# Moving the last flip of a projection next to another run of transposes, and putting the last rows' row sum on VectorE

## The chip, the cores and the metric

The kernel runs on one NeuronCore of a Trainium2 chip. The metric is the device time of one execution in microseconds, median over runs. Five engines work side by side, each through its own list of instructions in order: TensorE (PE, matmul), VectorE (DVE), ScalarE (ACT), GpSimd (POOL) and SyncE (SP, which issues most of the DMA transfers). They wait for one another by semaphores.

## The reference

A backbone of two layers over 512 tokens of width 1024, with 256 context tokens in front. Layer 0 mixes the tokens by bidirectional retention with 4 heads, layer 1 by a chunked gMLP; a final RMSNorm gives the output.

```
def rmsnorm(x, g):
    return x * rsqrt(mean(x * x, -1) + 1e-6) * g

for i in range(2):                       # 0: retention, 1: gMLP
    shift, scale, gate = split(silu(c) @ ada_w[i] + ada_b[i], 3)
    h = rmsnorm(x, norm_g[i]) * (1 + scale) + shift
    out = mixer_i(h, context)            # retention: (o_normed * silu(z)) @ w_out, o per head 512 wide
    x = x + gate * out
return rmsnorm(x, final_g)               # 512 x 1024
```

## The kernel before, in words

Every matrix product is done as three matmuls: each fp32 operand is split into a high and a low part, and `mm3` adds low x high, high x low and high x high in one PSUM tile. So there are 6820 matmul instructions.

Every engine operation goes through a recording class whose `call` stands in line 54, so nearly all rows of the profile bear the line L54; an operation is known by its engine and its tiles. The instructions stand on each engine in the order of the program text.

**PSUM.** `pt()` gives PSUM tiles (`pst`) from a set of six that are handed out in turn: the tile asked for now lies where the one asked for six calls earlier lay, and its first writer waits until the readers of that earlier one are done.

**The output projection of head 3** (`project_out`, called with `between=turned`, `prepare=prepare`, `then=half_sum`). The loop runs over two halves of the tokens (`hf`, 256 tokens each), four weight pieces (`c`) and two pieces of 128 output features each (`mi`; m = 2c + mi). Each m is one PSUM tile of 12 matmuls (`pst<-og,hl`), after which VectorE adds it, scaled by the gate, to the residual: `acc<-pst,gate,acc`. `og[hf]` is the head's gated output, transposed and split. For the first half it is ready when the loop begins; for the second half `flip()` makes it: 8 PE transposes of `gt` into two PSUM tiles, ScalarE's casts to the high part (`og<-pst`), and VectorE's two subtractions for the low part (`og<-pst,og`). In the kernel before, `flip()` stands ahead of c = 2 of the first half. `prepare()` stands right behind it in the text; it is elementwise work for layer 1's weights (`hl_e<-raw,hl_e` and `raw<-raw` on VectorE), with no matmul in it.

From c = 3 of the first half, `between(hf, c)` turns finished parts of the residual back to token rows: 8 PE transposes of `acc` into two PSUM tiles, whose squares ScalarE then sums (`junk<-pst`, `sums`) for layer 1's norm. These transposes need m = 0 to 3 of that half.

**The end.** The last matrix product is that of layer 1. Its last piece is row tile t = 3, columns 512 to 1023, and comes in two parts of 256 columns, c = 0 and 1. `last_part(t, c, pr)` adds each part to the residual, sums its squares for the RMSNorm, multiplies by the norm's weight (`fg`), and after c = 1 takes the root and the reciprocal, scales the tile's 1024 columns and stores them. `load` issues on SP's queue, `nc.scalar.dma_start` on ACT's.

Of the kernel before, what the change touches and what calls it, by code (L numbers as in the profile page):

```python
# [9 lines left out]
AF = mybir.ActivationFunctionType  # L10
ALU = mybir.AluOpType
# [15 lines left out]
HS = 256  # L27
# [40 lines left out]
def hybrid_kernel(ctx, tc, xT_d, cT_d, cv_d, sv_d, rows_d, ada0_d, adag_d, w_d, rope_d, dec_d, ws_d, id_d, out_d):  # L68
    nc = tc.nc
    pe, act, dve, sp = (Queue(tc, e) for e in (nc.tensor, nc.scalar, nc.vector, nc.sync))  # L70
# [11 lines left out]
    def st(shape, tag, dt=F32, bufs=1, name=None):  # L82
        return sb.tile(shape, dt, tag=tag, name=name or tag, bufs=bufs)
# [34 lines left out]
    def t2(name, shape=(P, 512), dt=F32):  # L118
        return st(list(shape), "t2", dt, bufs=T2, name=name)

    def pt(shape=(P, 512), tag="ps"):
        return ps.tile(list(shape), F32, tag=tag, name="pst", bufs=6 if tag == "ps" else 2)
# [3 lines left out]
    def mm3(out, l, r, first, last):  # L126
        (lh, ll), (rh, rl) = l, r
        mm(out, ll, rh, start=first, stop=False, skip_group_check=True)
        mm(out, lh, rl, start=False, stop=False, skip_group_check=True)
        mm(out, lh, rh, start=False, stop=last, skip_group_check=True)  # L130
# [13 lines left out]
    def load(dst, src):  # L144
        sp.dma_start(dst, src)
# [234 lines left out]
    def between_modes():  # L380

        pr = pt((P, P))
        mm(pr, ones, ones, start=True, stop=True)
# [678 lines left out]
    def aside(work):  # L1062
        return bound(lambda: next(work, None))

    def step():
        return aside(bg)
# [7 lines left out]
    def decay(h, tags=None):  # L1074

        if h == 1:
            xt, ct = st([P, XW], "s0", name="dt"), st([P, CW], "s2", name="dt")
        else:
            whole = st([P, TW], "dec", name="dt")
            xt, ct = whole[:, 0:XW], whole[:, XW:]  # L1080
        dts[h] = xt, ct
        if tags:
            tables[:] = [st([P, 768], tag, name="exps") for tag in tags]
            for t, parts in zip(tables, (((0, 384, 128), (2, 0, 384), (4, 256, 256)), ((2, 896, 128), (4, 512, 128), (0, 512, 512)))):
                o = 0
                for i, at, n in parts:
                    load(t[:, o:o + n], dec_d[i][:, at:at + n])
                    o += n
        yield
        up, down = tables  # L1090
        exp = lambda to, src, o: act.activation(to, src, AF.Exp, scale=lg[:, o + h:o + h + 1])
        free = lambda a, n: t2("de")[:, 0:n] if h == 2 else down[:, a:a + n]
        z = P * (NT - 1)
        exp(xt[:, z:z + P], up[:, 0:P], 0)
        m = free(z + 256, P)
        exp(m, down[:, z + 256:z + 256 + P], 4)
        dve.tensor_tensor(xt[:, z:z + P], xt[:, z:z + P], m, ALU.mult)
        dve.tensor_tensor(xt[:, z:z + P], xt[:, z:z + P], ident, ALU.add)
        exp(xt[:, 0:z], down[:, 256:256 + z], 4)
        exp(xt[:, z + P:], up[:, P:XW - z], 0)  # L1100
        yield
        exp(ct, up[:, P:], 0)
        for a, n in ((0, 512), (512, CW - 512)) if h == 2 else ((0, CW),):
            m = free(a, n)
            exp(m, down[:, a:a + n], 4)
            dve.tensor_tensor(ct[:, a:a + n], ct[:, a:a + n], m, ALU.add)
        act.activation(root, eps, AF.Sqrt)
        yield
# [10 lines left out]
    def load_qk(h):  # L1119
        tags = ODD if h in (1, 2) else EVEN  # L1120
        srcs = (k_d[h][0], q_d[h][0], k_d[h][1], kc_d[h], q_d[h][1])
        t = []
        for tag, src in zip(tags, srcs):
            t.append(st([P, 2, 2, HS], tag, F32R, name="qk"))
            load(f32(t[-1][:, 1]).rearrange("p a b -> p (a b)"), src)
            if len(t) % 2:
                yield
        qk[h] = (t[1], t[4]), (t[0], t[2]), t[3]
        for x in t:
            halves(x)  # L1130
            yield
# [28 lines left out]
    def load_v(h):  # L1160
        v = []
        for tag, src in zip(("oA11", "oS1", "oS2"), (*v_d[h], vc_d[h])):
            v.append(v_tile(h, tag))
            load(f32(v[-1][:, 1]), src)
            yield
        z = st([P, NT, 512], "oA22" if h == 1 else "oA12", name="z")
        for t in range(2):
            load(z[:, 2 * t:2 * t + 2, :], z_d[h][t])
        vv[h] = v, z
        yield  # L1170
        for x in v:
            halves(x)
            yield
# [283 lines left out]
    def project_out(ws, og, flip, parts, then=None, between=None, prepare=None):  # L1457
        for hf in range(2):
            sl = slice(hf * HS, hf * HS + HS)
            for c in range(4):  # L1460
                w = ws[c]
                if (hf, c) == (0, 2):
                    flip()
                    if prepare:
                        prepare()
                for work in parts:
                    aside(work)
                if then is None and (hf, c) in ((0, 3), (1, 0), (1, 2)):
                    step()
                for mi in range(2):  # L1470
                    m = 2 * c + mi
                    if between and mi == (hf == 1 and c < 2):
                        between(hf, c)
                    p = pt((P, HS))
                    for kk in range(4):
                        o = kk * 256 + mi * P
                        mm3(p, (w[:, 0, o:o + P], w[:, 1, o:o + P]), (og[hf][:, 0, kk, :], og[hf][:, 1, kk, :]), kk == 0, kk == 3)
                        if (hf, m, kk) == (0, 4, 1) and then is None:
                            between_modes()
                    dve.scalar_tensor_tensor(acc[:, m, sl], p, gate0[:, m:m + 1], acc[:, m, sl], ALU.mult, ALU.add)  # L1480
                    if then:
                        then(hf, m)
# [3 lines left out]
    flip, ss = attend_two(load_qk(1), load_v(1), decay(1, ("w3", "g1")), qs)  # L1486
# [9 lines left out]
    for work in own:  # L1496
        drained(work)
    project_out(wos.pop(2), og, flip, (decay(3), vs, qs))
    for c in range(4):
        nc.gpsimd.dma_start(acc[:, 2 * c:2 * c + 2, :], xT_d[:, 2 * c:2 * c + 2, :], accum_op=ALU.add)  # L1500
# [114 lines left out]
    def prepare():  # L1615
        Q.stage = 3
        Q.free += V1_SLOTS[len(W):] + [w for w in W if w not in Q.free]
        Q.pump()
        Q.upto(FIRST_V1 + 4)

    def turned(hf, c):
        first_half(hf, c)
        if hf == 1 and c >= 2:
            Q.upto(FIRST_V1 + 3 + c)

    project_out(wos.pop(HEADS - 1), og, flip, (), then=half_sum, between=turned, prepare=prepare)


# [45 lines left out]
    fg = st([P, D], "g0", name="fg")  # L1674
# [71 lines left out]
    def last_part(t, c, pr):  # L1746

        ss, o = ends[t]
        h = slice(512 + c * HS, 512 + c * HS + HS)
        s = o1[t][:, h]  # L1750
        dve.tensor_tensor(s, pr, s, ALU.add)
        act.activation(t2("junk1")[:, 0:HS], s, AF.Square, accum_out=ss[:, 1:2])
        if c == 0:
            dve.scalar_tensor_tensor(ss[:, 0:1], ss[:, 1:2], 1.0 / D, ss[:, 0:1], ALU.mult, ALU.add)
        dve.tensor_tensor(o[:, h], s, fg[:, h], ALU.mult)
        if c == 0:
            return
        rows = out_d[t * P:t * P + P, :]
        act.activation(ss[:, 1:2], ss[:, 1:2], AF.Sqrt, bias=ss[:, 0:1], scale=1.0 / D)
        dve.reciprocal(ss[:, 1:2], ss[:, 1:2])  # L1760
        act.activation(o[:, 768:], o[:, 768:], AF.Copy, scale=ss[:, 1:2])
        nc.scalar.dma_start(rows[:, 768:], o[:, 768:])
        for a in (slice(0, 384), slice(384, 768)):
            dve.tensor_scalar(o[:, a], o[:, a], ss[:, 1:2], None, ALU.mult)
            load(rows[:, a], o[:, a])

    vts = {}

# [177 lines left out]
```

## Time and profile before

| what | us |
|---|---|
| median of 3 runs (864.19, 864.30, 864.79) | 864.3 |
| profiled execution, its own time | 864.51 |
| its span, first to last instruction | 862.6 |
| PE busy | 851.6 (99%) |
| DVE busy | 705.9 (82%) |
| ACT busy | 479.7 (56%) |

All durations below are from that one profiled execution; 1.9 us of its time lie outside the span. Busy shares of engines that work side by side do not add up. PE's share is so high that the other engines matter in two ways alone: where PE waits for them, and after PE's last matmul.

### The profile page before, as it was taken

How to read it: one execution, taken by the hardware profiler on the slowest of the kernel's cores; microseconds unless marked ns; L12 is line 12 of the kernel's file. 1: busy time of each engine (PE TensorE's matmuls, PEld its weight loads, DVE VectorE, ACT ScalarE, POOL GpSimd, SP SyncE). 2: the span in 40 equal slices, each digit the busy share in tenths (PEclk: the TensorE clock that was granted, in tenths of full speed). 3: DMA queues.
4: the chain of work that ended last, by engine and by line, in shares of the span. 5: the costliest groups of instructions: out<-in, count | busy, mean ns of one | idle time of the engine just before them, and what ended most of it. 6: DMA issues, size and time to landing. Idle time of an engine off the chain costs nothing.

```text
span 862.6 us, 17054 instructions
## 1 busy us (share of the span) xinstructions
PE 851.6 (99%) x6820; PEld 814.4 (94%) x6820; DVE 705.9 (82%) x996; ACT 479.7 (56%) x763; POOL 84.9 (10%) x127
## 2 busy tenths in 40 slices
PE   8999999999999999999999999999999999999997
PEld 6899999999999999899999899999999899899985
DVE  4699899869977985799687889998888478678895
ACT  5466644455365356567872559754667456255434
POOL 0001211211211011000001011011000000000110
PEclk9999999999999999999999999999999999999999
DMA  9945858876967797247487842657556156156532
GB/s 356 404 130 154 246 173 251 267 212 188 313 209 232 219 317 246 74 122 232 162 273 187 258 110 99 221 158 235 157 147 209 36 148 220 26 152 190 122 46 101
DMA packets 78990, 164.03 MB, mean 190 GB/s; under 512 B 8256, under 2 KB 35264, under 8 KB 78912
## 3 DMA queue, kind: packets, MB, share of 16 engines
q1 hardware_dynamic: 66144, 122.37, 42.5%
q0 software_dynamic: 12336, 40.38, 18.6%
q8 instruction: 53, 0.87, 0.4%
q10 hardware_dynamic: 432, 0.20, 0.1%
q14 instruction: 25, 0.20, 0.1%
HBM read 124.65 MB, written 24.12 MB: 172 GB/s over the span
## 4 chain that ended last, share of the span: by engine, by line
PE 93%; DMA 3%; ACT 2%; DVE 1%; issue 0%; DVEq 0%; SPq 0%; ACTq 0%
PE pst L54 93%; DMA ada_w<-in_ada_dram 2%; DMA cq<-in_cT_dram 1%; DMA cv<-in_cv_dram 1%; DVE o L54 0%; ACT acc L54 0%; ACT junk L54 0%; ACT qk L54 0%; DVE hl L54 0%; ACT dt L54 0%; ACT L54 0%; DVE ada_h L54 0%; ACT og L54 0%; DVE snap L54 0%; ACT oA L54 0%
## 5 line engine op out<-in xcount | busy, mean ns | idle before, releaser
L54 DVE TENSOR_TENSOR hl<-raw,hl 128x1024 fp32r<-128x1024 f32 (+2 forms) x203 | 242.5, 1199 | 73.1 <-ACT hl L54 72.6
L54 ACT CAST hl<-raw 128x1024 fp32r<-128x1024 f32 (+2 forms) x203 | 208.4, 1031 | 143.0 <-PE pst L54 60.9
L54 PE MATMUL pst<-oS,hl 128*128 128x256 f32 x1296 | 154.7, 277 | 0.0
L54 PEld LDWEIGHTS pst<-oS,hl 128*128 128x128 f32 x1296 | 150.2, 188 | 0.9 <-issue 0.8
L54 PE MATMUL pst<-oA,hl 128*128 128x256 f32 x1080 | 134.3, 279 | 0.5 <-DVE hl L54 0.4
L54 PE MATMUL pst<-hl,oS 128*128 128x256 f32 x1152 | 134.7, 276 | 0.0
L54 PEld LDWEIGHTS pst<-hl,oS 128*128 128x128 f32 x1152 | 132.4, 188 | 0.8 <-issue 0.4
L54 PEld LDWEIGHTS pst<-oA,hl 128*128 128x128 f32 x1080 | 127.5, 188 | 2.6 <-issue 0.8
L54 PE MATMUL pst<-hl,oA 128*128 128x256 f32 x768 | 92.1, 277 | 0.0
L54 DVE TENSOR_TENSOR raw<-raw 128x1024 f32<-128x1024 f32 x73 | 88.9, 1219 | 0.8
L54 PEld LDWEIGHTS pst<-hl,oA 128*128 128x128 f32 x768 | 89.3, 188 | 0.0
L54 ACT ACTIVATE snap<-pst 128x512 f32<-128x512 f32 x81 | 48.2, 595 | 69.9 <-PE pst L54 69.8
L54 PE MATMUL pst<-v,ph 128*128 128x512 f32 x192 | 59.8, 393 | 0.0
L54 PE MATMUL pst<-hl,ya 128*128 128x512 f32 (+1 forms) x246 | 59.1, 386 | 0.0
L54 DVE TENSOR_TENSOR snap<-snap,pst 128x512 f32<-128x512 f32 x75 | 51.0, 680 | 4.5 <-PE pst L54 4.4
L187 POOL DMA_DIRECT2D raw<-raw x27 | 23.5, 869 | 315.3 <-DVE raw L54 207.0
L54 PEld LDWEIGHTS pst<-hl,ya 128*128 128x128 f32 x246 | 45.3, 188 | 9.5
L54 PE MATMUL pst<-og,hl 128*128 128x256 f32 x384 | 46.3, 280 | 0.0
L54 PEld LDWEIGHTS pst<-og,hl 128*128 128x128 f32 x384 | 45.0, 188 | 0.2
L54 PEld LDWEIGHTS pst<-v,ph 128*128 128x128 f32 x192 | 36.1, 188 | 7.0
L54 PE MATMUL pst<-v,pl 128*128 128x512 f32 x96 | 37.7, 393 | 0.0
L54 ACT CAST ph<-pf 128x512 fp32r<-128x512 f32 x24 | 14.9, 621 | 40.3 <-DVE pf L54 40.3
(225 smaller groups left out, 1101.1 us busy)
## 6 DMA issues: line engine op xcount, KB each, us to landing
raw<-in_w_dram SPq DMA_DIRECT2D x224, 256.0 KB, 3.8
bg<-in_adag_dram SPq DMA_DIRECT2D x32, 512.0 KB, 5.3
raw<-raw POOLq DMA_DIRECT2D x27, 512.0 KB, 5.2
ada_w<-in_ada_dram SPq DMA_DIRECT2D x16, 512.0 KB, 9.1
raw<-in_w_dram SPq DMA_DIRECT2D x16, 512.0 KB, 4.5
v<-snap POOLq DMA_DIRECT2D x16, 256.0 KB, 4.8
z<-snap POOLq DMA_DIRECT2D x16, 256.0 KB, 4.3
v<-v SPq DMA_DIRECT2D x8, 512.0 KB, 6.2
```

The lines of the kernel that those rows point to most:

```text
L54: made = op(*args, **kw)
L187: nc.gpsimd.dma_start(self.raws[q, to], self.raws[q, src], accum_op=ALU.add)
```

## The change

Two edits. In `project_out`, a call that has `between` (head 3 alone) now flips ahead of c = 3 of the first half and not ahead of c = 2; `prepare()` stays at c = 2. In `last_part`, the row sum of each 256-column part moves from ScalarE (Square with an accumulator) to one VectorE instruction with an accumulator; for the second part the multiply with `fg` is joined to the last scaling; and the three stores are cut another way: ACT's queue has columns 0 to 383, SP's has 384 to 767 and then 768 to 1023. Before, ACT's queue had the last 256 columns and SP's the two pieces of 384.

```diff
@@ project_out
-                if (hf, c) == (0, 2):
+                if (hf, c) == (0, 2) and prepare:
+                    prepare()
+                if (hf, c) == (0, 3 if between else 2):
                     flip()
-                    if prepare:
-                        prepare()
                 for work in parts:
                     aside(work)
@@ last_part
         dve.tensor_tensor(s, pr, s, ALU.add)
-        act.activation(t2("junk1")[:, 0:HS], s, AF.Square, accum_out=ss[:, 1:2])
+        dve.scalar_tensor_tensor(o[:, h], s, 1.0, s, ALU.mult, ALU.mult, accum_out=ss[:, 1:2])
         if c == 0:
             dve.scalar_tensor_tensor(ss[:, 0:1], ss[:, 1:2], 1.0 / D, ss[:, 0:1], ALU.mult, ALU.add)
-        dve.tensor_tensor(o[:, h], s, fg[:, h], ALU.mult)
-        if c == 0:
+            dve.tensor_tensor(o[:, h], s, fg[:, h], ALU.mult)
             return
         rows = out_d[t * P:t * P + P, :]
         act.activation(ss[:, 1:2], ss[:, 1:2], AF.Sqrt, bias=ss[:, 0:1], scale=1.0 / D)
         dve.reciprocal(ss[:, 1:2], ss[:, 1:2])
-        act.activation(o[:, 768:], o[:, 768:], AF.Copy, scale=ss[:, 1:2])
-        nc.scalar.dma_start(rows[:, 768:], o[:, 768:])
-        for a in (slice(0, 384), slice(384, 768)):
-            dve.tensor_scalar(o[:, a], o[:, a], ss[:, 1:2], None, ALU.mult)
-            load(rows[:, a], o[:, a])
+        act.activation(o[:, 0:384], o[:, 0:384], AF.Copy, scale=ss[:, 1:2])
+        nc.scalar.dma_start(rows[:, 0:384], o[:, 0:384])
+        dve.tensor_scalar(o[:, 384:768], o[:, 384:768], ss[:, 1:2], None, ALU.mult)
+        load(rows[:, 384:768], o[:, 384:768])
+        dve.scalar_tensor_tensor(o[:, h], s, ss[:, 1:2], fg[:, h], ALU.mult, ALU.mult)
+        load(rows[:, h], o[:, h])
```

On PE, in the first half of head 3's projection (`og,hl` are its products, 12 to an m; `ident,gt` the flip; `ident,acc` the residual's transposes):

```order
 L54 MATMUL pst<-ada_h,ones_r 128x512 x4
-L54 MATMUL pst<-og,hl 128x256 x48
-L54 MATMUL pst<-ident,gt 128x128 x8
-L54 MATMUL pst<-og,hl 128x256 x24
+L54 MATMUL pst<-og,hl 128x256 x72
+L54 MATMUL pst<-ident,gt 128x128 x8
 L54 MATMUL pst<-ident,acc 128x128 x8
 L54 MATMUL pst<-og,hl 128x256 x36
```

The flip's 8 transposes move behind the 24 products of c = 2 (m = 4 and 5), so that 16 transposes stand in a row. The 36 products behind them are m = 6, m = 7 and m = 0 of the second half. In the order in which PSUM tiles are asked for, m = 6 is the sixth after the flip's first tile in the kernel before, and the sixth after that of m = 4 in the changed one (m = 4, m = 5, two for the flip, two for `acc`, m = 6).

On DVE, at the same place (`acc<-pst` adds one m to the residual; `og<-pst,og` belongs to the flip; `hl_e` and `raw` to `prepare`):

```order
 L54 SCALAR_TENSOR_TENSOR acc<-pst,gate_895,acc 128x256
+L54 TENSOR_TENSOR hl_e<-raw,hl_e 128x1024 x2
+L54 TENSOR_TENSOR raw<-raw 128x1024
+L54 SCALAR_TENSOR_TENSOR acc<-pst,gate_895,acc 128x256 x2
 L54 TENSOR_TENSOR og<-pst,og 128x512 x2
-L54 TENSOR_TENSOR hl_e<-raw,hl_e 128x1024 x2
-L54 TENSOR_TENSOR raw<-raw 128x1024
-L54 SCALAR_TENSOR_TENSOR acc<-pst,gate_895,acc 128x256 x3
+L54 SCALAR_TENSOR_TENSOR acc<-pst,gate_895,acc 128x256
 L54 TENSOR_SCALAR sums<-sums 128x2
 L54 TENSOR_TENSOR raw<-raw 128x1024
```

The first row is m = 3, the three behind the old place of the flip are m = 4, 5 and 6. The flip's two subtractions move behind `prepare`'s three instructions and behind m = 4 and m = 5.

On DVE, at the program's end (`o_7530` is the residual of the last row tile, `o` its output, `fss` the sums):

```order
 L54 RECIPROCAL fss<-fss 128x1
-L54 TENSOR_TENSOR o<-o_7530,fg 128x256
+L54 SCALAR_TENSOR_TENSOR o,fss<-o_7530 128x256
 L54 TENSOR_SCALAR o<-o,fss 128x512
 L54 SCALAR_TENSOR_TENSOR fss<-fss 128x1
+L54 TENSOR_TENSOR o<-o_7530,fg 128x256
 L54 TENSOR_TENSOR o_7530<-pst,o_7530 128x256
-L54 TENSOR_TENSOR o<-o_7530,fg 128x256
+L54 SCALAR_TENSOR_TENSOR o,fss<-o_7530 128x256
 L54 RECIPROCAL fss<-fss 128x1
-L54 TENSOR_SCALAR o<-o,fss 128x384 x2
+L54 TENSOR_SCALAR o<-o,fss 128x384
+L54 SCALAR_TENSOR_TENSOR o<-o_7530,fss,fg 128x256
```

Each part's square is now VectorE's own, the first part's multiply with `fg` stands ahead of the second part's add all the same, and the last instruction is a product of three factors over 256 columns.

## Rows read from the trace of the kernel before

**Rows 1.** The page, part 1: busy time, share of the span, instructions.

```profile
PE 851.6 (99%) x6820; PEld 814.4 (94%) x6820; DVE 705.9 (82%) x996; ACT 479.7 (56%) x763; POOL 84.9 (10%) x127
```

**Rows 2.** Chain of waits, core 0: start, length, what (x pieces merged).

```profile
494.77 356.15 PE pst L54 x2753
...
858.50 0.33 DVEq L1942
```

**Rows 3.** Timeline of PE, head 3's projection: start, us, engine, line, operation.

```profile
495.58 5.82 PE L54 MATMUL pst<-og,hl 128*128 128x256 f32 x48
501.23 1.04 PE L54 MATMUL pst<-ident,gt 128*128 128x128 f32 x8
502.02 2.99 PE L54 MATMUL pst<-og,hl 128*128 128x256 f32 x24
504.85 1.04 PE L54 MATMUL pst<-ident,acc 128*128 128x128 f32 x8
505.64 4.49 PE L54 MATMUL pst<-og,hl 128*128 128x256 f32 x36
```

**Rows 4.** Timeline of DVE, same stretch (in brackets: idle before, and its releaser).

```profile
502.71 1.28 DVE L54 TENSOR_TENSOR og<-pst,og 128x512 fp32r<-128x512 f32 x2
503.91 2.35 DVE L54 TENSOR_TENSOR hl_e<-raw,hl_e 128x1024 fp32r<-128x1024 f32 x2
506.18 1.22 DVE L54 TENSOR_TENSOR raw<-raw 128x1024 f32<-128x1024 f32 x1
507.31 1.26 DVE L54 SCALAR_TENSOR_TENSOR acc<-pst,gate,acc 128x256 f32<-128x256 f32 x3
```

**Rows 5.** Timeline of PE, 48 products further on.

```profile
595.20 5.61 PE L54 MATMUL pst<-hl,oA 128*128 128x256 f32 x48
```

**Rows 6.** Windows: busy time and count of PE, clock, DMA share, GB/s.

```profile
538.66:602.77 64.11, 64.11 (x568) 1.00 0.67 206
```

**Rows 7.** Timeline of DVE and ACT, the program's end.

```profile
855.54 0.84 PE L54 MATMUL pst<-hl,yc 128*128 128x256 f32 x6
...
855.72 0.41 DVE L54 TENSOR_TENSOR o<-o,fg 128x256 f32<-128x256 f32 x1
855.94 0.19 ACT L54 ACTIVATION_READ_ACCUMULATOR junk<-o 128x1 f32 x1
856.03 0.71 ACT L54 ACTIVATE o<-o,fss 128x512 f32<-128x512 f32 x1
856.04 0.48 DVE L54 TENSOR_SCALAR o<-o,fss 128x512 f32<-128x512 f32 x1
856.44 0.15 DVE L54 SCALAR_TENSOR_TENSOR fss<-fss 128x1 f32<-128x1 f32 x1
856.50 0.42 DVE L54 TENSOR_TENSOR o<-pst,o 128x256 f32<-128x256 f32 x1
856.96 0.42 DVE L54 TENSOR_TENSOR o<-o,fg 128x256 f32<-128x256 f32 x1
...
857.56 0.29 ACT L54 ACTIVATE fss<-fss 128x1 f32<-128x1 f32 x1
857.88 0.16 DVE L54 RECIPROCAL fss<-fss 128x1 f32<-128x1 f32 x1 [0.50 <-ACT fss L54]
858.08 0.51 ACT L54 ACTIVATE o<-o,fss 128x256 f32<-128x256 f32 x1 [0.23 <-DVE fss L54]
858.08 0.75 DVE L54 TENSOR_SCALAR o<-o,fss 128x384 f32<-128x384 f32 x2
```

**Rows 8.** Groups of DVE by shape, whole span: busy, mean ns of one, idle before.

```profile
L54 DVE SCALAR_TENSOR_TENSOR acc<-pst,gate,acc 128x256 f32<-128x256 f32 x32 | 14.5, 477 | 4.6 <-PE pst L54 4.5
...
L54 DVE SCALAR_TENSOR_TENSOR xs<-xs 128x512 f32<-128x512 f32 x4 | 2.7, 686 | 0.0
L54 DVE TENSOR_TENSOR xs<-xs 128x512 f32<-128x512 f32 x4 | 2.6, 686 | 0.0
```

**Rows 9.** DMA issues in 857 to 862.6: count, KB each, median us to landing.

```profile
out_dram<-o SPq DMA_DIRECT2D x2, 192.0 KB, 2.1
```

## The prediction

> **What bounds the kernel now.** First the page's busy times [rows 1]: PE works in 851.6 of the span's 862.6 us, every other engine much less, so a change counts where PE waits or after PE is done. Then the chain of waits [rows 2]: from 494.77 one piece of 356.15 us is PE alone, to 850.92; no wait for another engine or a transfer breaks it. Behind it the chain goes through DVE and ACT to the last stores, issued from 858.50 on. Both edits lie on this chain: the flip at 501 to 506, inside the unbroken piece, so that PE time lost there has nothing behind it that gives it back; and the last rows, where every step counts. The span ends at 862.6, some 4 us behind the first of the last issues: that is store latency and the program's end, which I take as fixed. Then the two timelines of PE and DVE from 495 to 510 [rows 3, 4] and the one of the end [rows 7] give the terms.
>
> **The moved flip: what PE itself does.** PE runs the same instructions in another order: 48 products, 8 + 8 transposes and 24 products end where m = 6 begins, at 505.64 [rows 3], whichever order they stand in. The 16 transposes now stand side by side, which removes one passage from transposes to products. A set of 8 takes 0.79 from its first start to the first product's (501.23 to 502.02), close to 8 times a tenth, so there is no pause that joining them could save. I cost that at 0.
>
> One small thing can shift: PE runs products of this shape at two paces. The 48 of this place take 5.82, 48 further on 5.61 [rows 5]: 0.21, or 4.4 ns for each. Here the two paces alternate from stretch to stretch: 36 products take 1.50 more than 24 (4.49 against 2.99), and 12 more at the pace of the quicker 48 would be 12 x 5.61 / 48 = 1.40, at the pace of the slower 1.46; so the 24 run at the quicker pace and the 36 at the slower one. Joined to the 48, the 24 should keep the slower pace: +24 x 4.4 ns = +0.1. The next 36, and a like 36 behind them, could change to the quicker one: down to -0.3. Between -0.3 and +0.1 I take 0 for the net, but keep it in mind that m = 6 may come up to 0.1 later.
>
> **The moved flip: what PE then waits for.** The new wait is on a PSUM tile. Tiles come from a set of six in turn. Before, the tile of m = 6 was the flip's first, which DVE had read in the `og` subtraction from 502.71 on; by 505.64 that was long over. Now it is the tile of m = 4, which is free when DVE has added m = 4 to the residual. On DVE that addition stands behind `prepare`'s three instructions, and DVE is busy without a gap here [rows 4]: two `hl_e` from 503.91 to 506.18 (2.27, start to start), `raw` from 506.18 to 507.31 (1.13), then m = 4. With the two `og` subtractions moved behind it (502.71 to 503.91, 1.20), the addition starts at 507.31 - 1.20 = 506.11 and lasts 0.48 [rows 8]: it ends at 506.59. PE is ready at 505.64. So PE waits 0.95; if it comes 0.1 later by its own slower pace, 0.85. I take **+0.9**, with 0.7 to 1.1 as bounds.
>
> Behind that wait I look at what is late next. The `og` subtractions now start when m = 5 has been added, 506.11 + 2 x 0.39 = 506.89 (three additions take 1.26, so 0.39 from one to the next), and end at about 508.2. Their first reader is m = 0 of the second half, behind the 24 products of m = 6 and 7: 506.6 + 24 x 0.118 = 509.4. ScalarE's casts for them follow the flip and have the same time. So no second wait; 1.2 of cover is left. The addition of m = 5, whose tile m = 7 needs, ends at 506.98, and m = 7 begins 12 products behind m = 6, at 508.0. The transposes of `acc` (504.85 before) need m = 0 to 3 alone, and those stand ahead of the moved work. If `prepare`'s three instructions did not stand in front of m = 4, the term would be nothing: that is the step on which it hangs.
>
> **The end: what goes.** Before [rows 7]: PE is done with the last part at 856.38; DVE comes to its addition only at 856.50, behind the first part's `fg` multiply, a 512-column scaling and the small sum. From there 1.06 to the root on ACT (857.56), 0.32 to the reciprocal (857.88), 0.20 to the two scalings of 384 (858.08 to 858.83), and the last store is issued right behind.
>
> What the change adds: the first part's square takes the place at 855.72 and the `fg` multiply still stands ahead of the addition, so DVE has one instruction more in front of it. Its price: an instruction of this size with two SBUF inputs holds DVE for 0.32 (855.72 to 856.04), and the accumulator has to be written out. No row of DVE shows that. On ACT, reading an accumulator is an instruction of 0.19, and the next starts 0.09 behind it (855.94 to 856.03). Between 0 and 0.19 I take 0.09. So the addition starts 0.41 later, at 856.91, PE long being done.
>
> From the addition to the root: a dependent DVE instruction starts 0.46 behind it (856.50 to 856.96), lasts 0.42, and its accumulator 0.09; the hop to ACT adds some 0.05, as for the other hops. That makes 1.02 against 1.06: ACT's own square and accumulator are gone, DVE's are in their place. -0.04.
>
> From the reciprocal on: 0.20 to the scaling of 384 on DVE, 0.33 for that one (half of 0.75 less overlap), then the three-factor product over 256. With a pointer scalar such an instruction takes 0.48 [rows 8]. End at +0.20 + 0.33 + 0.48 = 1.01 behind the reciprocal's start + 0.0 against 0.95 (857.88 to 858.83) before: +0.06. ACT's 384 columns lie between its 0.51 for 256 and 0.71 for 512, so 0.61, and are done before that.
>
> The stores: three on two queues, as before; 192 KB land 2.1 after the issue [rows 9]. The last one is now 128 KB instead of 192, while ACT's grew to 192 and goes out some 0.1 to 0.2 ahead of it. Together they move the same bytes. Between -0.2 (a smaller last store) and 0, I take -0.1. The end then costs 0.41 - 0.04 + 0.06 - 0.1 = **+0.33**.
>
> **The sum.** 0.9 + 0 + 0.33 = +1.23. The profiled execution's own time would go from 864.51 to 865.74; the runs' median is 0.21 below that execution, so I forecast **865.5**. With the terms' bounds (0.7 to 1.1; -0.3 to +0.1; 0.1 to 0.6) the likeliest case spans 864.8 to 866.1.
>
> **Rivals.**
>
> *The accumulating square runs at half speed.* A 256-column instruction would then cost what one of 512 does, 0.686 in place of 0.42 [rows 7, 8]: +0.27, and two of them stand one behind the other on the path (the first part's delays the addition, the second's the root): +0.54, so 866.0. Against it: the four `xs` instructions of the same kind with two fp32 SBUF inputs take 0.686 over 512 columns, exactly as the plain two-input ones do [rows 8]. But none of those has an accumulator, so the rows don't exclude it. [...] The `xs` rows show no halving without an accumulator. Chance 0.14.
>
> *The slower pace stays.* The pace of a stretch of products seems to be set where it begins, and the change alters what stands before those that follow. PE has 568 instructions without a break from 538.66 to 602.77 [rows 6], 64.11 us, at 0.113 each, the quicker pace. If these fell to the slower, 565 x 4.4 ns = +2.5 on top of the sum: 868.0, clearly slower. It decides from about 120 products on, since +0.5 more crosses the bound. Against it: several other small sets of PE work lie between the change and 538, each of which can set the pace anew. Chance 0.06.
>
> *No new wait worth the name.* If DVE's order were kept but its work got done sooner, or the pace came back with its full -0.3 and the tail cost nothing, as when the squares on DVE hide under the time that PE's last part takes, the sum is 0.9 - 0.3 + 0 = +0.6 at most and 0 at least: 864.3 to 864.9. Against it: DVE has no gap from 502 to 508, and the addition at 856.50 already lies behind PE's end. Chance 0.15.
>
> *A gain.* The end could come out shorter if the hop from DVE to ACT and ACT's accumulator cost more than the rows show and the smaller last store landed much sooner (-0.5 or more), with the wait absent: 862.6 or less would need another 1.2 that I see nowhere. Chance 0.02.
>
> The sum as above has the remaining 0.63.
>
> **How the numbers follow.** What a measurement of this kernel can tell from no change is about 0.2%, 1.7 us: faster is below 862.6, slower above 866.0. The likeliest case lies within it but for its upper edge (0.03 of its 0.63); half speed lies at the bound (0.09 of 0.14 above, as the other terms may be above theirs too); the slower pace is all above (0.06). Slower 0.18, faster 0.02, same 0.80. The range leaves out the slower pace and the gain: from 864.4, the third case's lower half cut, to 866.4, half speed with the wait at its upper bound.
>
> **What would show it.** Step one: in the changed trace PE stands idle for 0.9 ahead of the 36 products behind the 16 transposes, released by DVE's `acc`, and the chain of waits breaks there. It is wrong if m = 6 begins within 0.2 of 505.64. Step two: the second 256-column addition starts some 0.4 later behind PE's end, DVE's square takes 0.42 and not 0.69, and the last issue comes 0.3 to 0.4 later. Step three: the products from 538 to 603 take 64.1 us as before; 66.6 would be the slower pace.

## The result, and the profile after

The changed kernel takes 865.49 us (median of 22 runs, 864.74 to 866.92), the kernel before 864.27 (22 runs beside them, 863.47 to 865.72): a ratio of 1.0014, 95% interval 1.0008 to 1.0021. That is 1.2 us or 0.14% slower, and 865.5 was forecast. The profiled execution took 865.36, its span is 863.4.

The timeline of PE in the changed kernel, head 3's projection (start, us, operation; in brackets the idle time before and what ended it), answers to [rows 3]:

```profile
495.51 8.34 PE L54 MATMUL pst<-og,hl 128*128 128x256 f32 x72
503.69 1.03 PE L54 MATMUL pst<-ident,gt 128*128 128x128 f32 x8
504.56 1.04 PE L54 MATMUL pst<-ident,acc 128*128 128x128 f32 x8
506.17 4.37 PE L54 MATMUL pst<-og,hl 128*128 128x256 f32 x36 [0.57 <-DVE acc L54]
...
539.00 0.38 PE L54 MATMUL pst<-ones 128*128 128x128 f32 x2
```

There is the forecast wait, ahead of m = 6 and released by VectorE's addition. Without it m = 6 would have followed the second set of transposes as it did before, 0.79 behind its start, at 505.35; it starts 0.82 later. (The bracket says 0.57, since it counts from the end of the last transpose, 505.60; without a wait that end overlaps what follows, in [rows 3] 504.85 + 1.04 = 505.89 against a next start at 505.64.) VectorE at the same time, answering to [rows 4]:

```profile
502.24 2.35 DVE L54 TENSOR_TENSOR hl_e<-raw,hl_e 128x1024 fp32r<-128x1024 f32 x2
504.50 1.22 DVE L54 TENSOR_TENSOR raw<-raw 128x1024 f32<-128x1024 f32 x1
505.64 0.87 DVE L54 SCALAR_TENSOR_TENSOR acc<-pst,gate,acc 128x256 f32<-128x256 f32 x2
506.43 1.28 DVE L54 TENSOR_TENSOR og<-pst,og 128x512 fp32r<-128x512 f32 x2
```

The addition of m = 4 starts at 505.64 behind `prepare`'s three instructions, ends at 506.13, and PE goes on 0.04 behind that. The chain of waits, one piece from 494.77 to the end before [rows 2], now has that addition in it:

```profile
494.71 10.90 PE pst L54 x91
505.64 0.49 DVE acc L54
506.13 0.04 issue
506.17 345.24 PE pst L54 x2662
```

The end (timeline of PE, DVE and ACT) answers to [rows 7]:

```profile
856.02 0.84 PE L54 MATMUL pst<-hl,yc 128*128 128x256 f32 x6
...
856.19 0.41 DVE L54 SCALAR_TENSOR_TENSOR o<-o 128x256 f32<-128x256 f32 x1
...
856.52 0.08 DVE L54 DVE_READ_ACCUMULATOR o<-o 128x1 f32 x1
856.52 0.48 DVE L54 TENSOR_SCALAR o<-o,fss 128x512 f32<-128x512 f32 x1
856.92 0.15 DVE L54 SCALAR_TENSOR_TENSOR fss<-fss 128x1 f32<-128x1 f32 x1
856.99 0.42 DVE L54 TENSOR_TENSOR o<-o,fg 128x256 f32<-128x256 f32 x1
857.33 0.42 DVE L54 TENSOR_TENSOR o<-pst,o 128x256 f32<-128x256 f32 x1
857.78 0.42 DVE L54 SCALAR_TENSOR_TENSOR o<-o 128x256 f32<-128x256 f32 x1
858.13 0.08 DVE L54 DVE_READ_ACCUMULATOR o<-o 128x1 f32 x1
858.25 0.29 ACT L54 ACTIVATE fss<-fss 128x1 f32<-128x1 f32 x1 [1.21 <-DVE o L54]
858.57 0.16 DVE L54 RECIPROCAL fss<-fss 128x1 f32<-128x1 f32 x1 [0.36 <-ACT fss L54]
858.77 0.61 ACT L54 ACTIVATE o<-o,fss 128x384 f32<-128x384 f32 x1 [0.23 <-DVE fss L54]
858.77 0.42 DVE L54 TENSOR_SCALAR o<-o,fss 128x384 f32<-128x384 f32 x1
859.11 0.48 DVE L54 SCALAR_TENSOR_TENSOR o<-o,fss,fg 128x256 f32<-128x256 f32 x1
```

The second addition starts 1.31 behind PE's last piece of six products (856.02 to 857.33), before 0.96 (855.54 to 856.50). The order is as forecast: the first square, the `fg` multiply and then the addition.

**One table for all profiles.** One execution differs from the next by several tenths before anything that was changed, so I compare stretches and not whole times. All are differences of starts in the PE timelines: A from head 3's first product to the `ones` pair at 538.52 (before: 495.58 to 538.52); B from there to the `ones` pair at 602.77; C from that pair to the last six products (855.54); D from those to the span's end (862.6; the span is given to a tenth, so that D is good to some 0.05). The two `ones` pairs of the kernel before:

```profile
538.52 0.38 PE L54 MATMUL pst<-ones 128*128 128x128 f32 x2
...
602.77 0.39 PE L54 MATMUL pst<-ones 128*128 128x128 f32 x2
```

| kernel (profile) | A | B | C | D |
|---|---|---|---|---|
| before | 42.94 | 64.25 | 252.77 | 7.06 |
| e9, e10: before, again | 42.91, 42.97 | 64.24, 64.24 | 252.77, 252.77 | 7.12, 7.13 |
| changed | 43.49 | 64.24 | 252.78 | 7.38 |
| e8, e12: changed, again | 43.49, 43.50 | 64.24, 64.24 | 253.39, 252.78 | 7.42, 7.42 |
| e1: flip alone | 44.07 | 64.24 | 253.77 | 7.14 |
| e2, e11: end alone | 42.94, 43.21 | 64.24, 64.24 | 252.77, 252.77 | 7.41, 7.40 |
| e3, e7: other tile | 42.91, 42.92 | 64.31, 64.30 | 252.81, 253.20 | 7.40, 7.38 |
| e4: end, fg late | 43.15 | 64.24 | 252.78 | 7.05 |
| e5: prepare behind | 43.05 | 64.24 | 253.11 | 7.40 |
| e6: more ahead | 47.25 | 64.25 | 252.77 | 7.44 |

In the three profiles of each kernel the changed one is 0.55 longer in A and 0.30 longer in D: 0.85 of the 1.2.

### The profile page after: what moved, and what is told of

Same layout as the page of the kernel before. It is cut to its first block, busy times and chain, and to the rows that moved or that the text cites. A ratio compares the mean times of both kernels' runs of the same rounds, so it can differ in the third digit from the quotient of the medians.

```text
span 863.4 us, 17049 instructions
## 1 busy us (share of the span) xinstructions
PE 852.1 (99%) x6820; PEld 814.0 (94%) x6820; DVE 706.7 (82%) x999; ACT 478.9 (55%) x759; POOL 84.8 (10%) x127
## 4 chain that ended last, share of the span: by engine, by line
PE 93%; DMA 3%; ACT 2%; DVE 1%; issue 0%; DVEq 0%; SPq 0%; ACTq 0%
PE pst L54 93%; DMA ada_w<-in_ada_dram 2%; DMA cq<-in_cT_dram 1%; DMA cv<-in_cv_dram 1%; DVE o L54 0%; ACT acc L54 0%; ACT qk L54 0%; ACT junk L54 0%; DVE hl L54 0%; ACT dt L54 0%; ACT L54 0%; DVE ada_h L54 0%; DVE snap L54 0%; ACT og L54 0%; ACT oA L54 0%
```

## The experiments

**e1: the flip alone.** The changed kernel with the old `last_part`.

```diff
-    changed last_part
+    last_part as before
```

> The moved flip alone, the end as before. Theory (two separate costs): PE waits 0.6 to 0.9 us ahead of m = 6 for VectorE's addition of m = 4, PE's last piece ends 0.5 to 0.9 later than before, and from PE's end to the last store's issue nothing changes; time +0.6 to +0.9 over the kernel before. Rival (the pace of the products moved, not a wait): no idle time of PE ahead of m = 6, the same products take longer. Rival (the end alone costs): time as before, within 0.2.

Measured: 865.23 us (11 runs), ratio 1.0013 (1.0004 to 1.0022). Its timeline of PE:

```profile
495.38 8.64 PE L54 MATMUL pst<-og,hl 128*128 128x256 f32 x72
...
504.74 1.04 PE L54 MATMUL pst<-ident,acc 128*128 128x128 f32 x8
506.60 4.37 PE L54 MATMUL pst<-og,hl 128*128 128x256 f32 x36 [0.83 <-DVE acc L54]
```

The wait is there without the new end, 506.60 against 504.74 + 0.79: 1.07, A is 1.1 longer, D as before. It is longer than in the changed kernel because VectorE is later: its addition of m = 4 starts 10.69 behind head 3's first product (506.07 against 495.38), in the changed kernel 10.13 (505.64 against 495.51). What puts VectorE late shows on ACT, in the first `hl_e` cast, whose weight piece must have landed; the kernel before, e1 and the changed kernel:

```profile
493.91 1.05 ACT L54 CAST hl_e<-raw 128x1024 fp32r<-128x1024 f32 x1 [0.45 <-DMA raw<-in_w_dram]
```

```profile
493.87 1.05 ACT L54 CAST hl_e<-raw 128x1024 fp32r<-128x1024 f32 x1 [0.60 <-DMA raw<-in_w_dram]
```

```profile
493.44 1.05 ACT L54 CAST hl_e<-raw 128x1024 fp32r<-128x1024 f32 x1
```

Before, the cast waits 0.45 for the transfer, in e1 0.60, in the changed kernel not at all; behind the cast stand ScalarE's sums of head 3, behind these VectorE's `gt`, `gateb` and additions. The other profiles bear it out (e6 apart, which has an instruction more there). Where the cast doesn't wait (five of them, all three of the changed kernel among these), VectorE's addition of m = 3 starts 6.2 to 6.3 us behind head 3's first product; with a wait of 0.25 to 0.27 (e5, e7) it starts 6.5 to 6.6 behind it, and with one of 0.44 to 0.68 (the kernel before in all its profiles, e1, e4, e11) 6.7 to 7.0. So the size of the term hangs on a landing that differs from run to run.

**e2: the end alone.** The kernel before with the changed `last_part`.

```diff
-    last_part as before
+    changed last_part
```

> The changed end alone, the flip as before. Theory: PE's timeline as before; the second 256-column addition starts 0.35 to 0.45 us later behind PE's end, the last store is issued 0.2 to 0.4 later; time +0.3. Rival (the accumulating square at half speed): the 256-column square takes 0.69 and the time is +0.8. Rival (the flip alone costs): time as before.

Measured: 864.39, ratio 1.0003 (0.9994 to 1.0012). In the time this can't be told from nothing, or from +0.3; in the profile D is 7.41 against 7.06, and 7.40 in a second profile, while A stays within the scatter of the kernel before and C is the same. The square takes 0.41 to 0.43, not 0.69.

**e3 and e7: another PSUM tile.** Both edits; one of the two tiles of the residual's first transposes is taken from the other set, so that m = 6 gets the tile of m = 3.

```diff
-            pq = pt()
+            pq = pt(tag="tm") if (hf, g, i) == (0, 0, 0) else pt()
```

> Both edits, but the first of the two tiles of the residual's first transposes comes from the other PSUM set (two tiles), so that m = 6 gets the tile of m = 3 and not that of m = 4. PE's order and VectorE's stay as in the changed kernel. Theory: m = 6 begins right behind the 16 transposes, the 0.5 to 0.9 are gone, time +0.3 over before (the end's part). Rival (the order on PE or its pace costs): time as the changed kernel, +1.2.

Measured: 865.43, ratio 1.0017 (1.0008 to 1.0026). The timeline of PE:

```profile
504.46 1.04 PE L54 MATMUL pst<-ident,gt 128*128 128x128 f32 x8
505.33 1.04 PE L54 MATMUL pst<-ident,acc 128*128 128x128 f32 x8
506.12 2.08 PE L54 MATMUL pst<-og,hl 128*128 128x256 f32 x16
```

VectorE's additions of m = 4 and m = 5:

```profile
505.96 0.86 DVE L54 SCALAR_TENSOR_TENSOR acc<-pst,gate,acc 128x256 f32<-128x256 f32 x2
```

With the order of both engines unchanged the wait is gone (506.12 is 0.79 behind 505.33) and A is 42.91, as before. The addition of m = 4 is still late, it starts at 505.96, but m = 6 no longer needs its tile. The 72 products took 8.65 here and 8.34 in the changed kernel, so the pace doesn't explain the longer A of the latter either. That shows that the loss in A is this one PSUM tile, and neither the order on PE nor its pace. But the time did not fall, against my theory. So I ran it again for a second profile.

> The kernel with one of the transposes' tiles from the other PSUM set once more, for a second profile: in its first one head 3's stretch lost nothing, yet its time was +1.1. Theory: the wait is gone for good, and what its other executions lost is lost later, where a short wait of PE for a PSUM tile sets it to its slower pace (0.118 for 0.113 us a product) for some 200 products, about +1.0 in some executions. Rival: the first profile was a lucky execution, and in most the wait at m = 6 is there; then the second profile shows it.

Measured: 865.31, ratio 1.0012 (1.0003 to 1.002), single runs from 864.01 to 867.28. A is 42.92 again: the first profile was no lucky execution. C is 0.43 longer here. Where C grows stands under e8 to e12. A, C and D together explain some 0.4 and 0.7 over before in the two profiles; the other part of the 1.1 lies ahead of head 3's projection or in executions without a profile, and stays open. (Head 3's first product starts between 494.6 and 496.1 us in the 14 profiles, at 495.3 on average without the moved flip and at 495.4 with it.)

**e4: the fg multiply late.** The kernel before with the changed end, and the first part's `fg` multiply forced behind the second part's square. (The order on VectorE isn't simply that of the text, as the section on the kernel has it: in [rows 7] the first part's `fg` multiply, at 855.72, runs ahead of the small sum, at 856.44, that stands in front of it in the text. `pinned` holds an instruction behind the one in front of it in the text.)

```diff
-            dve.tensor_tensor(o[:, h], s, fg[:, h], ALU.mult)
             return
...
+        dve.pinned = True
+        dve.tensor_tensor(o[:, 512:768], o1[t][:, 512:768], fg[:, 512:768], ALU.mult)
+        dve.pinned = False
         dve.reciprocal(ss[:, 1:2], ss[:, 1:2])
```

> The changed end alone, with the first part's fg multiply forced behind the second part's square on VectorE, where that engine waits for the root anyway. Theory (the end's cost is one more instruction ahead of the second addition): the addition starts at most 0.1 us later than before, the last issue within 0.1 of before's; time +0.0 to +0.1. Rival (the square on VectorE or the three-factor product at the end costs): time +0.3 as with the changed end.

Measured: 864.44, ratio 1.0003 (0.9995 to 1.0012). Its end on PE and DVE:

```profile
855.35 0.84 PE L54 MATMUL pst<-hl,yc 128*128 128x256 f32 x6
```

```profile
856.32 0.42 DVE L54 TENSOR_TENSOR o<-pst,o 128x256 f32<-128x256 f32 x1
856.77 0.42 DVE L54 SCALAR_TENSOR_TENSOR o<-o 128x256 f32<-128x256 f32 x1
...
857.12 0.42 DVE L54 TENSOR_TENSOR o<-o,fg 128x256 f32<-128x256 f32 x1
857.57 0.16 DVE L54 RECIPROCAL fss<-fss 128x1 f32<-128x1 f32 x1
```

The addition starts 0.97 behind PE's last piece, as before (0.96), and D is 7.05. The multiply now lies in the time in which VectorE waits for the root. So the whole cost of the end, 0.30 to 0.35, is the one instruction more ahead of the addition; square, accumulator, three-factor product and the new cut of the stores together cost nothing that D shows.

**e5: prepare behind the flip.** Both edits, `prepare` called at c = 3.

```diff
-                if (hf, c) == (0, 2) and prepare:
-                    prepare()
                 if (hf, c) == (0, 3 if between else 2):
                     flip()
+                    if prepare:
+                        prepare()
```

> Both edits, with prepare called behind the flip at c = 3, so that VectorE adds m = 4 and m = 5 behind only one hl_e instruction and not behind three. Theory (PE waits for the PSUM tile of m = 4, late by VectorE's queue): no idle time of PE ahead of m = 6, the stretch from head 3's first product to 36 products later as long as before within 0.1; left is the end's cost, time +0.1 to +0.3 over before. Rival (the order on PE, or what the moved flip does later in the program, costs): time as the changed kernel, +1.2.

Measured: 864.9, ratio 1.0008 (0.9999 to 1.0016). VectorE, then PE:

```profile
502.03 1.22 DVE L54 TENSOR_TENSOR hl_e<-raw,hl_e 128x1024 fp32r<-128x1024 f32 x1
503.17 1.10 DVE L54 SCALAR_TENSOR_TENSOR acc<-pst,gate,acc 128x256 f32<-128x256 f32 x2
504.19 1.22 DVE L54 TENSOR_TENSOR hl_e<-raw,hl_e 128x1024 fp32r<-128x1024 f32 x1
```

```profile
505.25 4.35 PE L54 MATMUL pst<-og,hl 128*128 128x256 f32 x36
```

Only one `hl_e` stands ahead of m = 4, whose tile is free before 505.25 (the additions of m = 4 and m = 5 are both done at 504.27), and PE doesn't wait: A is 43.05. A second way to take the wait away, this time by VectorE's order with the tiles as in the changed kernel. The time is 0.7 over before, where +0.1 to +0.3 was expected; the interval holds both. In the profile the excess is in C, which is 0.34 longer, as in some of the others.

**e6: more ahead of the addition.** Both edits, and two VectorE instructions on a tile that is unused at that time.

```diff
+                    dve.pinned = True
+                    dve.tensor_scalar(quarter["21"], quarter["21"], 0.0, None, ALU.mult)
+                    dve.pinned = False
...
+    dve.memset(quarter["21"], 0.0)
```

> Both edits, and two more VectorE instructions of 1024 columns (a memset ahead of m = 0's addition, a scaling between prepare and m = 4's addition) that compute nothing used. Theory: each microsecond that they hold VectorE ahead of m = 4 is a microsecond more of PE's wait, about 1.0 in all: PE waits 1.6 to 2.0 ahead of m = 6 and the time is +1.0 over the changed kernel, +2.2 over before. Rival (the wait is covered later, or isn't the cost): time within 0.3 of the changed kernel.

Measured: 868.38, ratio 1.0048 (1.0035 to 1.006), 4.2 over before where the theory had 2.2. From head 3's first product (494.59) to m = 6 (507.39) it takes 12.80, in the changed kernel 10.66: 2.14 more. The two instructions hold VectorE for 0.82 and 0.60; a later landing, as in e1 (the cast waits 0.62 here), makes up most of the rest. So the wait follows VectorE's queue about one for one. A is 3.76 longer than in the changed kernel; the other 1.6 of that come behind the wait (the timeline of PE, then windows of PE: busy time and count, granted clock, DMA share, GB/s):

```profile
507.39 5.98 PE L54 MATMUL pst<-og,hl 128*128 128x256 f32 x36 [2.71 <-DVE acc L54]
```

```profile
495.00:503.60 8.60, 8.60 (x78) 1.00 0.41 125
503.60:507.39 3.79, 1.08 (x10) 1.00 0.00 0
507.39:511.00 3.61, 3.61 (x17) 0.53 0.75 145
511.00:513.20 2.20, 2.20 (x21) 1.00 0.04 7
```

Behind 2.71 of idle time the granted clock is 0.53 in the 3.61 us from 507.39 to 511.00 and 1.00 again from 511.00 to 513.20; the 36 products take 5.98 and not 4.37. Behind the changed kernel's 0.57 of idle time the clock stays at 1.00 (window 506.17 to 510.30). My expectation had left the clock out.

**e8 to e12: more profiles.** The same kernels again, since the stretch C differed.

> The changed kernel once more, for a second profile. Theory: PE waits 0.5 to 0.9 ahead of m = 6, by how late the weight piece for prepare's first cast lands, and everything up to PE's last matmul is as much later as that wait says; from PE's last matmul to the end +0.3.

> The kernel before, a second profile. In five of the seven profiles with the moved flip PE waited some 0.04 to 0.1 us at about 649 for a PSUM tile that ScalarE frees behind a late vt load, and ran slower behind it; in none of the three without. Theory (chance: the load lands between 5.1 and 5.8 us in any kernel): one or more of the profiles without the moved flip shows the late load too. Rival (the moved flip makes the load late): all profiles without it have it at 5.1.

> The kernel before, a third profile, with the same two expectations for the vt load at about 640 and for PE's products from 640 to 688.

> The changed end alone, a second profile: the same two expectations for the vt load; and from PE's last matmul to the end +0.3 as in its first profile.

> The changed kernel, a third profile. PE's stretch around head 3's projection is 0.5 to 1.1 longer than before, by how late VectorE comes to its queue there, and the end 0.3 longer. Theory (chance): the vt load may be at 5.1 or later. Rival (the moved flip makes it late): later than 5.1 in most.

Measured, one run each: 865.22, 864.57, 863.95, 864.57 and 865.89. A and D of the changed kernel repeat within 0.05 (43.49, 43.49, 43.50; 7.38, 7.42, 7.42). C is 252.77 or 252.78 in all six profiles without the moved flip, and longer, by 0.03 to 1.0, in five of the eight with it. The kernel before, run once beside the last four, took 866.20, so that a microsecond between two single runs means little.

What makes C longer stands in the traces of e5, e7 and e8: a late load of `vt`, for which ACT waits and with it PE. The chain of waits of e8, and the PE row at its end:

```profile
639.90 5.80 DMA vt<-vt
...
647.83 0.50 ACT snap L54
...
648.37 202.90 PE pst L54 x1416
```

```profile
648.37 3.02 PE L54 MATMUL pst<-oS,hl 128*128 128x256 f32 x24 [0.32 <-ACT snap L54]
```

ACT normalizes `vt` once it has landed, and only behind that it empties a PSUM tile (`snap<-pst`) that PE needs. In the six profiles without the moved flip ACT waits 0.76 to 0.89 for the load, and PE doesn't notice. What it waits beyond that comes out in C: 0.93 makes C 0.04 longer (e3), 1.22 makes it 0.34 (e5), 1.32 makes it 0.43 (e7) and 1.48 makes it 0.62 (e8). Behind the wait PE goes on at the pace of the kernel before (the 96 `ya` products take 22.14 in e3, e5, e7 and e8, as there). The expectations of e7 and e9 have a wait of at most 0.1 and a slower pace behind it; the slower pace is there in e1 alone. There ACT waits 0.99, the 48 products of PE beside it take 5.80 and not 5.60, and from there PE goes on at its slower pace to the end of the `ya` products:

```profile
646.37 5.80 PE L54 MATMUL pst<-oS,hl 128*128 128x256 f32 x48
652.01 2.99 PE L54 MATMUL pst<-oA,hl 128*128 128x256 f32 x24
654.83 5.11 PE L54 MATMUL pst<-oS,hl 128*128 128x256 f32 x42
...
665.09 22.56 PE L54 MATMUL pst<-hl,ya 128*128 128x512 f32 x96
```

Before, the three groups behind the 48 take 2.88, 4.92 and 22.14. What dropped the pace in e1 isn't shown.

Why the load is late is open. It landed in 5.1 to 5.2 in the six profiles without the moved flip, in 5.1 to 5.8 in the eight with it, and chance would rarely divide the profiles so. But the chip is a rival that nothing here excludes: the three latest loads, 5.5 to 5.8 in e5, e7 and e8, all come from one chip, and of the runs whose chip is known only kernels with the moved flip were profiled on it (e6, from the same chip, has 5.1). On each of the two chips on which both kinds were profiled (e1 to e4, e9 to e12) the load landed in 5.1 to 5.2 without the moved flip and in 5.2 to 5.3 with it. And nothing that I found in the traces leads from the flip at 504 to a load 140 us later. Whether the moved flip makes C longer is open.

## Why the prediction was right, and where it was not

**Joined transposes save nothing: right.** The second set starts 0.87 behind the first and m = 6, without a wait (e3), 0.79 behind that; A without the wait is 42.91 and 42.92, as before.

**The wait on m = 4's tile: right, mis-sized by 0.35 in A.** It was forecast at +0.9 and is +0.55 in each profile of the changed kernel, +1.1 in e1 and at most 0.1 in e3, e5 and e7, which take away nothing but the tile or VectorE's order. The step that was off is the start of VectorE's queue: I took its times from one execution, in which the cast ahead of it waited 0.45 for a landing, as a fixed schedule. In the three profiles of the changed kernel it didn't wait, and VectorE was 0.4 earlier against PE in the first of them (what follows m = 3's addition starts 6.73 behind head 3's first product, 502.24 against 495.51; before 7.13 [rows 3, 4]). The durations behind that start were as forecast. One part of PE's pace went the other way: the 24 products, joined to the 48, were to keep the slower pace, but in the changed kernel's profiles all 72 ran at the quicker one (8.34; in e1, e3, e5 and e7 8.64 or 8.65). PE was ready 0.2 earlier by that and gained nothing, since it waits for VectorE: the wait is 0.82 long, but m = 6 is only 0.60 later than before, counted from head 3's first product. Behind the wait the two stretches of 36 take 4.37 and 4.35 (before both 4.49), the 24 take 3.07 (2.98), inside the bound of -0.3 to +0.1; at the end of A 0.05 of that is left.

**No second wait behind it: right.** The 36 products run through in 4.37; `og` was done at 507.71, a microsecond and more ahead of its reader.

**The end: right in sum, +0.30 in D for +0.33.** The addition came 0.35 later (forecast 0.41: the accumulator's read, 0.08, and the next instruction both start at 856.52, where I had put 0.09 between them); from the addition to the root 0.92 (1.02); from the reciprocal to the end of the last scaling 1.02 against 0.95 (+0.07 for +0.06); and the smaller last store brought nothing, where I had -0.1: its 128 KB landed 2.4 behind the issue, the 192 KB before 2.1 [rows 9].

**The rivals.** Half speed of the accumulating square: out, with 0.42 for 256 columns where 0.69 was its price. The slower pace from 538 to 603: out, B is 64.24 or 64.25 in all but e3 and e7 (64.31, 64.30); the slower pace did stay for a long stretch once, in C of e1. No new wait, and a gain: out. The prediction took 0.2% as the least that can be told from no change; 22 runs on each side told 0.14% from none (0.08% to 0.21%).

The total came out at 1.2 for 1.23 partly by luck: A and D, with the steps shown by e1 to e6, hold 0.85. The rest lies in the scatter of single executions, in C among others (0, 0.6 and 0 in the three profiles of the changed kernel), and isn't settled. In whole times the wait can't be seen to go: e3 and e7, without it, are 1.1 over before and e5 is 0.7, the changed kernel 1.2. So the wait is shown as the cause of the longer A, and not of the whole 1.2. No version beat both kernels by what can be measured: e4's end is level with the old one, and the flip at its new place brings nothing that could be kept, even without the wait.

## What to carry to other kernels

When a step that takes tiles from a rotating set moves, count anew which tile each later step gets: the products that were moved ahead gave their own late tile to the next ones, and the engine that must empty it had three long instructions in front (3.40 us, from 502.24 to 505.64). An instruction may be free in one place of a short tail and cost its time in another (the `fg` multiply of the first part: D is 7.05 in e4 and 7.41 in e2); put what nobody waits for into the time in which its engine waits anyway. And a wait worked out from one profile inherits that execution's landings: look for a transfer that ended an idle time upstream (here a wait of 0 to 0.68 from profile to profile), and give the term the width of it.

## What the runs showed of the hardware that was not expected

The same products on the same operands run at two paces in different executions of one program, with the granted clock at 1.00 at both: the first 48 of head 3 took 5.82 in the first profile of the kernel before and 5.62 in e9, the 72 took 8.34 in the changed kernel and 8.64 in e1. In e1 PE fell to the slower pace in mid-stretch, at 646 to 652, where nothing of the program changed, and kept it to 687: 1.0 us in all. In e5, e7 and e8 ACT, and with it PE, waited longer at that place (ACT 1.22 to 1.48, in e1 0.99), and PE didn't fall. What sets the pace isn't settled.

Behind an idle time of 2.71 us, ahead of which PE had done 16 transposes, the granted clock was 0.53 for 3.6 us (e6, one profile); behind one of 0.57 at the same place it was 1.00 (the changed kernel).
